# Huber loss on one core: the pair's target tile in parts of 8704 and 7680 columns instead of two rows

## The chip, the cores and the metric

The kernel runs on one core of a Trainium2 chip. The time of a run is the device time in microseconds (us). VectorE is called DVE in the profile and ScalarE ACT; SP is SyncE, which here only issues DMA transfers, and SPq is its queue of instructions. GB/s are 10^9 bytes a second, MB are 10^6 bytes; the profile's KB are 1024 bytes, so that 4096.0 KB are 4.19 MB.

## The reference

Two float32 arrays of 8192 x 8192 come in, one of the same shape goes out:

```python
def reference(pred, target):
    delta = 1.0
    diff = pred - target
    abs_diff = np.abs(diff)
    return np.where(abs_diff <= delta, 0.5 * diff**2, delta * (abs_diff - 0.5 * delta))
```

With d = pred - target the kernel computes max(|d| - 0.5, 0.5 * clip(d, -1, 1)**2), which is the same. Each input is read once and the output is written once: 536.87 MB in and 268.44 MB out.

## The kernel before

The 8192 rows are cut into 32 steps. A step has 256 rows, two neighbouring rows to each of the 128 partitions, so that a partition's share of a step lies in one run of 16,384 numbers (64 KB) in the DRAM. Step i's prediction is loaded into one of two buffers of that size, `pairs[i % 2]`. Its target is loaded into two buffers of one row each (8192 columns, 32 KB a partition): `rows[0]` for the even row, `rows[1]` for the odd one; there is only one of each, so the next step's target row can be loaded only when the present step's compute on it is over. The result is written over the prediction and stored from there as one transfer of 8.39 MB.

`compute(i, r, widths)` works on one row in pieces of columns. For each piece, DVE subtracts the target from the prediction in place (line 80, `tensor_tensor`) and writes the clipped difference over the target (line 81, `tensor_scalar`); ACT squares that with a scale (line 84) and takes the absolute value of the difference in place (line 85); DVE finishes with `max(|d| - 0.5, square)` (line 74, `scalar_tensor_tensor`). The list `todo` and `finish(2)` hold the last operation back by two pieces, so that DVE has subtracts to do while ACT works; `finish(0)` at the row's end does what is left. The pieces of an even row are `EVEN` (two of 4096 columns), those of an odd row `ODD` (4096, 2048, 2048), and both rows of the last step use `FINE` (four of 2048).

All transfers are issued by SP, and the order of the program is the order written by hand (`tc.manual_schedule()`, line 90). SP issues one after the other and stands still at one whose condition isn't met, with all later ones behind it. In the steady state, one step issues four transfers in this order:

- `load_row(i, 1)` (line 58): the odd target row of step i. It waits until step i-1's compute on `rows[1]` is over.
- `load_pair(i + 1)` (line 50): the next step's prediction. It waits until the store of step i-1, which used the same buffer, has ended.
- `load_row(i + 1, 0)` (line 58): the next even target row. It waits for step i's compute on `rows[0]`.
- `store_pair(i)` (line 61): it waits for step i's compute on its odd row.

Near the end the order differs a little. The last prediction is loaded a row at a time (lines 103 and 109, `load_pred_row`, line 54). The last odd target row is loaded in four pieces of 2048 columns (line 110), each of which waits only for the compute on its own columns. Then come the store of step 30 (line 112), that of the last step's even row (line 113) and four stores of 2048 columns of its odd row (line 114, `store_row`, line 66). At the start (lines 92 to 95), the first even row's prediction and target are loaded in two pieces each.

Of the kernel before, what the change touches and what calls it, by code (L numbers as in the profile page):

```python
# [1 line left out]

# [4 lines left out]


@with_exitstack
def kernel(  # L10
    ctx: ExitStack,
    tc: tile.TileContext,
    pred: bass.AP,
    target: bass.AP,
    out: bass.AP,
):
    nc = tc.nc
    P = 128
    R = 2
    fp32 = mybir.dt.float32  # L20
    Alu = mybir.AluOpType
    Act = mybir.ActivationFunctionType
    SQRT_HALF = 0.70710678118654752

    n_rows, W = pred.shape
    pred_t = pred.rearrange("(n p r) m -> n p (r m)", p=P, r=R)
    targ_t = target.rearrange("(n p r) m -> n p (r m)", p=P, r=R)
    out_t = out.rearrange("(n p r) m -> n p (r m)", p=P, r=R)
    n = pred_t.shape[0]

    pool = ctx.enter_context(tc.tile_pool(name="slots", bufs=1))
    pairs = [pool.tile([P, R * W], fp32, name=f"pair{k}") for k in range(2)]
    rows = [pool.tile([P, W], fp32, name=f"row{k}") for k in range(R)]

    EVEN = [4096, 4096]
    ODD = [4096, 2048, 2048]
    FINE = [2048, 2048, 2048, 2048]

    def cuts(widths):
        out_, at = [], 0  # L40
        for w in widths:
            out_.append(slice(at, at + w))
            at += w
        return out_

    def at_row(r, c):
        return slice(r * W + c.start, r * W + c.stop)

    def load_pair(i):
        nc.sync.dma_start(out=pairs[i % 2], in_=pred_t[i, :, :])  # L50

    def load_pred_row(i, r):
        c = slice(r * W, (r + 1) * W)
        nc.sync.dma_start(out=pairs[i % 2][:, c], in_=pred_t[i, :, c])  # L54

    def load_row(i, r, widths=None):
        for c in cuts(widths or [W]):
            nc.sync.dma_start(out=rows[r][:, c], in_=targ_t[i, :, at_row(r, c)])  # L58

    def store_pair(i):  # L60
        nc.sync.dma_start(out=out_t[i, :, :], in_=pairs[i % 2])  # L61

    def store_row(i, r, widths):
        for c in cuts(widths):
            ca = at_row(r, c)
            nc.sync.dma_start(out=out_t[i, :, ca], in_=pairs[i % 2][:, ca])

    def compute(i, r, widths):
        todo = []

        def finish(keep):
            while len(todo) > keep:
                a, b = todo.pop(0)
                nc.vector.scalar_tensor_tensor(  # L74
                    out=a, in0=a, scalar=-0.5, in1=b, op0=Alu.add, op1=Alu.max
                )

        for c in cuts(widths):
            a, b = pairs[i % 2][:, at_row(r, c)], rows[r][:, c]
            nc.vector.tensor_tensor(out=a, in0=a, in1=b, op=Alu.subtract)  # L80
            nc.vector.tensor_scalar(  # L81
                out=b, in0=a, scalar1=-1.0, scalar2=1.0, op0=Alu.max, op1=Alu.min
            )
            nc.scalar.activation(out=b, in_=b, func=Act.Square, scale=SQRT_HALF)  # L84
            nc.scalar.activation(out=a, in_=a, func=Act.Abs)  # L85
            todo.append((a, b))
            finish(2)
        finish(0)

    ctx.enter_context(tc.manual_schedule())  # L90

    for c in cuts(EVEN):
        nc.sync.dma_start(out=pairs[0][:, c], in_=pred_t[0, :, c])  # L93
        nc.sync.dma_start(out=rows[0][:, c], in_=targ_t[0, :, c])  # L94
    load_pred_row(0, 1)
    for i in range(n):
        last = i == n - 1
        if not last:
            load_row(i, 1)
            if i + 1 < n - 1:  # L100
                load_pair(i + 1)
            else:
                load_pred_row(i + 1, 0)
        compute(i, 0, EVEN if not last else FINE)
        if not last:
            load_row(i + 1, 0)
        compute(i, 1, ODD if not last else FINE)
        if i + 1 == n - 1:
            load_pred_row(i + 1, 1)
            load_row(i + 1, 1, FINE)  # L110
        if not last:
            store_pair(i)
    store_row(n - 1, 0, [W])
    store_row(n - 1, 1, FINE)


# [1 line left out]
_INS = ['pred', 'target']  # L118
_OUTS = [((8192, 8192), 'float32')]


# [23 lines left out]
```

## Time and profile before

| | us |
|---|---|
| median of 3 runs | 1877.39 |
| lowest and highest of them | 1874.84, 1877.78 |
| the profiled execution's own time | 1877.36 |
| its span | 1875.6 |
| ACT busy | 912.9 (49%) |
| SP's line 61 (store) waiting for DVE, in total | 798.2 |
| SP's line 50 (pair load) waiting for the store of two steps ago, in total | 710.6 |
| SP's line 58 (target load) waiting for DVE, in total | 227.6 |
| DVE waiting for a target load (line 80), in total | 306.7 |
| ACT waiting for DVE (line 84), in total | 948.5 |

The span is that of one execution, taken by the hardware profiler; the time of the same execution has 1.8 us more around it. Waiting times of different engines overlap, and a wait costs time only where nothing else is busy meanwhile. "DMA" in a view's row is the mean busy share of the core's 16 DMA engines; in short stretches it can pass 1.00, as a transfer's packets are counted where they begin.

The durations by operation and width (partitions x columns), which the prediction uses:

| line, operation | 128x4096, ns | 128x2048, ns |
|---|---|---|
| 80 TENSOR_TENSOR | 4423 | 2283 |
| 81 TENSOR_SCALAR | 2294 | 1226 |
| 84 ACTIVATE (square) | 3611 | 1894 |
| 74 SCALAR_TENSOR_TENSOR (STT) | 4424 | 2287 |

### The profile page before, as it was taken

To read this page: it belongs to the slowest core of one execution; us is meant where nothing else is said; L and a number is where in the kernel's file an instruction comes from. 1 tells how busy PE (TensorE), PEld (TensorE's weight loads), DVE (VectorE), ACT (ScalarE), POOL (GpSimd) and SP (SyncE) were. 2 spreads that over 40 slices of the span, in tenths; PEclk is the share of its full clock that TensorE was granted. 3 is DMA by queue.
4 is the path that set the end of the run, shared out by engine and by line. 5 is a ranking of instruction groups with operands and counts; after the bars stand their busy time and mean duration, and the time that the engine had idled before them with its cause. 6 is when DMAs were issued, how large, how long until landed. Compare 5 with 4: busy or idle time off the path is not lost.

```text
span 1875.6 us, 1196 instructions
## 1 busy us (share of the span) xinstructions
DVE 1430.2 (76%) x489; ACT 912.9 (49%) x327; POOL 0.2 (0%) x4
## 2 busy tenths in 40 slices
DVE  5777877778777787777877778777787777877787
ACT  3635536355364553644535445354453544535455
POOL 0000000000000000000000000000000000000000
DMA  9999999999999999999999999999999999999999
GB/s 425 414 436 435 438 425 429 439 428 431 440 425 442 429 429 442 419 434 443 417 436 432 439 425 426 425 442 427 428 428 442 424 427 443 418 435 423 428 425 386
DMA packets 20025, 805.39 MB, mean 429 GB/s; under 512 B 2224, under 2 KB 2224, under 8 KB 2224
## 3 DMA queue, kind: packets, MB, share of 16 engines
q1 hardware_dynamic: 20016, 805.32, 99.9%
q14 instruction: 9, 0.07, 0.0%
HBM read 536.87 MB, written 268.44 MB: 429 GB/s over the span
## 4 chain that ended last, share of the span: by engine, by line
DMA 57%; ACT 24%; DVE 17%; SPq 1%; issue 0%; DVEq 0%
DMA row<-in_target_dram 57%; ACT row L84 12%; ACT pair L85 12%; DVE pair L80 8%; DVE pair L74 4%; DVE row L81 4%; SPq L61 1%; DVEq L140 0%; SPq L94 0%; SPq L93 0%; SPq L58 0%; SPq L54 0%; DVEq L80 0%
## 5 line engine op out<-in xcount | busy, mean ns | idle before, releaser
L84 ACT ACTIVATE row<-row 128x4096 f32<-128x4096 f32 (+1 forms) x163 | 468.4, 2874 | 948.5 <-DVE row L81 948.5
L80 DVE TENSOR_TENSOR pair<-pair,row 128x4096 f32<-128x4096 f32 (+1 forms) x163 | 571.1, 3504 | 306.7 <-DMA row<-in_target_dram 306.7
L74 DVE SCALAR_TENSOR_TENSOR pair<-pair,row 128x4096 f32<-128x4096 f32 (+1 forms) x163 | 568.7, 3507 | 122.4 <-ACT pair L85 122.4
L85 ACT ACTIVATE pair<-pair 128x4096 f32<-128x4096 f32 (+1 forms) x163 | 467.4, 2867 | 0.0
L81 DVE TENSOR_SCALAR row<-pair 128x4096 f32<-128x4096 f32 (+1 forms) x163 | 299.1, 1835 | 5.6
L84 ACT ACT_TABLE_LOAD x1 | 1.3, 1283 | 0.7 <-PEq L129 0.7
L129 POOL MEMSET const-bfloat16-1.0<- 128x1 bf16 x1 | 0.1, 101 | 0.0
L129 POOL MEMSET const-uint8-127<- 128x1 uint8 x1 | 0.1, 101 | 0.0
L129 POOL MEMSET const-float32-0.0<- 128x1 f32 x1 | 0.1, 98 | 0.2 <-issue 0.2
L129 POOL MEMSET const-float32-1.0<- 128x1 f32 x1 | 0.1, 98 | 0.0
## 6 DMA issues: line engine op xcount, KB each, us to landing
row<-in_target_dram SPq DMA_DIRECT2D x62, 4096.0 KB, 33.9
pair<-in_pred_dram SPq DMA_DIRECT2D x3, 4096.0 KB, 29.7
pair<-in_pred_dram SPq DMA_DIRECT2D x2, 2048.0 KB, 11.6
row<-in_target_dram SPq DMA_DIRECT2D x2, 2048.0 KB, 16.1
row<-in_target_dram SPq DMA_DIRECT2D x4, 1024.0 KB, 15.7
out_dram<-pair SPq DMA_DIRECT2D x1, 4096.0 KB, 22.5
out_dram<-pair SPq DMA_DIRECT2D x4, 1024.0 KB, 9.5
out_dram<-pair SPq DMA_DIRECT2D x31, 25.3
```

Source lines behind the costliest of these rows:

```text
L61: nc.sync.dma_start(out=out_t[i, :, :], in_=pairs[i % 2])
L74: nc.vector.scalar_tensor_tensor(out=a, in0=a, scalar=-0.5, in1=b, op0=Alu.add, op1=Alu.max)
L80: nc.vector.tensor_tensor(out=a, in0=a, in1=b, op=Alu.subtract)
L81: nc.vector.tensor_scalar(out=b, in0=a, scalar1=-1.0, scalar2=1.0, op0=Alu.max, op1=Alu.min)
L84: nc.scalar.activation(out=b, in_=b, func=Act.Square, scale=SQRT_HALF)
L85: nc.scalar.activation(out=a, in_=a, func=Act.Abs)
L129: nc = _bacc.Bacc("TRN2", target_bir_lowering=False, num_devices=1)
```

## The change

The target's two buffers are no longer one row each. The pair of rows, which is one run of 16,384 columns, is cut at column 8704: part 0 has 8704 columns and part 1 has 7680. `targs[0]` and `targs[1]` have these sizes, 65,536 bytes a partition together as before. Compute goes by parts: part 0 in two pieces of 4352 columns, part 1 in pieces of 3840, 1920 and 1920; the last step in four pieces of 2176 and four of 1920. The pair buffers, the prediction loads and the stores of steps 0 to 29 stay as they were. In the last step the prediction comes in the two parts, the target's part 1 as one transfer instead of four, part 0 is stored as one transfer and part 1 in four of 1920 columns. The loop runs to the last step but one, and the last step's compute stands behind it.

```diff
+    CUT = 8704
+    part = [slice(0, CUT), slice(CUT, R * W)]
+    COARSE = [[4352, 4352], [3840, 1920, 1920]]
+    FINE = [[2176] * 4, [1920] * 4]
+
     pool = ctx.enter_context(tc.tile_pool(name="slots", bufs=1))
     pairs = [pool.tile([P, R * W], fp32, name=f"pair{k}") for k in range(2)]
-    rows = [pool.tile([P, W], fp32, name=f"row{k}") for k in range(R)]
+    targs = [
+        pool.tile([P, p.stop - p.start], fp32, name=f"targ{k}") for k, p in enumerate(part)
+    ]
 
-    EVEN = [4096, 4096]
-    ODD = [4096, 2048, 2048]
-    FINE = [2048, 2048, 2048, 2048]
...
+    def load_targ(i, k, widths=None):
+        for ca, cb in cuts(k, widths or [part[k].stop - part[k].start]):
+            nc.sync.dma_start(out=targs[k][:, cb], in_=targ_t[i, :, ca])
...
-    def compute(i, r, widths):
+    def compute(i, k, widths):
...
-        for c in cuts(widths):
-            a, b = pairs[i % 2][:, at_row(r, c)], rows[r][:, c]
+        for ca, cb in cuts(k, widths):
+            a, b = pairs[i % 2][:, ca], targs[k][:, cb]
...
-    for c in cuts(EVEN):
-        nc.sync.dma_start(out=pairs[0][:, c], in_=pred_t[0, :, c])
-        nc.sync.dma_start(out=rows[0][:, c], in_=targ_t[0, :, c])
-    load_pred_row(0, 1)
-    for i in range(n):
-        last = i == n - 1
-        if not last:
-            load_row(i, 1)
-            if i + 1 < n - 1:
-                load_pair(i + 1)
-            else:
-                load_pred_row(i + 1, 0)
-        compute(i, 0, EVEN if not last else FINE)
-        if not last:
-            load_row(i + 1, 0)
-        compute(i, 1, ODD if not last else FINE)
-        if i + 1 == n - 1:
-            load_pred_row(i + 1, 1)
-            load_row(i + 1, 1, FINE)
-        if not last:
-            store_pair(i)
-    store_row(n - 1, 0, [W])
-    store_row(n - 1, 1, FINE)
+    whole = slice(0, R * W)
+    for ca, cb in cuts(0, COARSE[0]):
+        load_pred(0, ca)
+        nc.sync.dma_start(out=targs[0][:, cb], in_=targ_t[0, :, ca])
+    load_pred(0, part[1])
+    for i in range(n - 1):
+        near_end = i + 1 == n - 1
+        load_targ(i, 1)
+        load_pred(i + 1, part[0] if near_end else whole)
+        compute(i, 0, COARSE[0])
+        load_targ(i + 1, 0)
+        compute(i, 1, COARSE[1])
+        if near_end:
+            load_pred(i + 1, part[1])
+            load_targ(i + 1, 1)
+        store(i, whole)
+    for k in range(2):
+        compute(n - 1, k, FINE[k])
+    store(n - 1, part[0])
+    for ca, _ in cuts(1, FINE[1]):
+        store(n - 1, ca)
```

`cuts(k, widths)` now gives each piece's columns twice, counted in the pair and in the part; `load_pred(i, c)` and `store(i, c)` move the columns `c` of a pair buffer.

More of the change, by code (lines that the diff above doesn't have):

```diff
@@ L29, with cuts, load_pred, store @@
     n = pred_t.shape[0]
+    CUT = 8704
+    part = [slice(0, CUT), slice(CUT, R * W)]
+    COARSE = [[4352, 4352], [3840, 1920, 1920]]
+    FINE = [[2176] * 4, [1920] * 4]
     pool = ctx.enter_context(tc.tile_pool(name="slots", bufs=1))
     pairs = [pool.tile([P, R * W], fp32, name=f"pair{k}") for k in range(2)]
-    rows = [pool.tile([P, W], fp32, name=f"row{k}") for k in range(R)]
-    EVEN = [4096, 4096]
-    ODD = [4096, 2048, 2048]
-    FINE = [2048, 2048, 2048, 2048]
-    def cuts(widths):
-        out_, at = [], 0
+    targs = [
+        pool.tile([P, p.stop - p.start], fp32, name=f"targ{k}") for k, p in enumerate(part)
+    ]
+    def cuts(k, widths):
+        at, found = 0, []
         for w in widths:
-            out_.append(slice(at, at + w))
+            found.append((slice(part[k].start + at, part[k].start + at + w), slice(at, at + w)))
             at += w
[L44 to L53, printed above, removed]
-        nc.sync.dma_start(out=pairs[i % 2][:, c], in_=pred_t[i, :, c])
[L56 to L63, printed above, removed]
-        for c in cuts(widths):
-            ca = at_row(r, c)
-            nc.sync.dma_start(out=out_t[i, :, ca], in_=pairs[i % 2][:, ca])
-    def compute(i, r, widths):
+        return found
+    def load_pred(i, c):
+        nc.sync.dma_start(out=pairs[i % 2][:, c], in_=pred_t[i, :, c])
+    def load_targ(i, k, widths=None):
+        for ca, cb in cuts(k, widths or [part[k].stop - part[k].start]):
+            nc.sync.dma_start(out=targs[k][:, cb], in_=targ_t[i, :, ca])
+    def store(i, c):
+        nc.sync.dma_start(out=out_t[i, :, c], in_=pairs[i % 2][:, c])
+    def compute(i, k, widths):
         todo = []
@@ L76, in finish @@
                 )
-        for c in cuts(widths):
-            a, b = pairs[i % 2][:, at_row(r, c)], rows[r][:, c]
+        for ca, cb in cuts(k, widths):
+            a, b = pairs[i % 2][:, ca], targs[k][:, cb]
             nc.vector.tensor_tensor(out=a, in0=a, in1=b, op=Alu.subtract)
```

## The prediction

> **What bounds the kernel now.** I read the page's head first, to see which engine is full.
>
> ```profile
> span 1875.6 us, 1196 instructions
> DVE 1430.2 (76%) x489; ACT 912.9 (49%) x327; POOL 0.2 (0%) x4
> ...
> DMA  9999999999999999999999999999999999999999
> ...
> q1 hardware_dynamic: 20016, 805.32, 99.9%
> ```
>
> The 16 DMA engines have work for 99.9% of the span; VectorE (DVE) has a quarter of it free. The page's chain blames target loads for 57% and compute for most of the rest, but a chain only follows what released what: a load that lands 34 us after its issue was queued most of that time. So I asked for stretches: all steps, then a quick step and a long one, then the end (columns: stretch, its length, three engines' busy time with counts, clock, DMA share, GB/s).
>
> ```profile
> 65.60:1820.10 1754.50, 1340.91 (x451) 853.78 (x300) 0.00 (x0) 1.00 1.00 431
> ```
>
> ```profile
> 592.20:650.20 58.00, 44.68 (x15) 28.46 (x10) 0.00 (x0) 1.00 1.00 432
> 650.20:709.40 59.20, 44.68 (x15) 28.46 (x10) 0.00 (x0) 1.00 1.00 434
> ```
>
> ```profile
> 1868.00:1870.00 2.00, 0.00 (x0) 0.00 (x0) 0.00 (x0) 1.00 1.00 422
> 1870.00:1872.00 2.00, 0.00 (x0) 0.00 (x0) 0.00 (x0) 1.00 0.53 221
> 1872.00:1874.00 2.00, 0.00 (x0) 0.00 (x0) 0.00 (x0) 1.00 0.15 61
> ```
>
> Compute is identical in short and long steps; only the stream's length differs. The DMA engines stay full to 1870 us, five microseconds after the last compute, and then stop one by one over some 4 us: they don't run level, and the last one sets the end. Last, the timeline of one step, to see how early each transfer is queued (start, duration, engine, line; in brackets the idle time before it).
>
> ```profile
> 1702.38 0.34 SPq L61 DMA_DIRECT2D out_dram<-pair  x1
> 1702.83 0.37 SPq L58 DMA_DIRECT2D row<-in_target_dram  x1
> 1709.23 4.42 DVE L80 TENSOR_TENSOR pair<-pair,row 128x4096 f32<-128x4096 f32 x1 [6.87 <-DMA row<-in_target_dram]
> ...
> 1728.50 0.33 SPq L50 DMA_DIRECT2D pair<-in_pred_dram  x1
> ...
> 1734.63 0.33 SPq L58 DMA_DIRECT2D row<-in_target_dram  x1
> 1738.20 4.42 DVE L80 TENSOR_TENSOR pair<-pair,row 128x4096 f32<-128x4096 f32 x1 [3.59 <-DMA row<-in_target_dram]
> ...
> 1761.66 0.34 SPq L61 DMA_DIRECT2D out_dram<-pair  x1
> ```
>
> Transfers run in the order SyncE (SP) issued them. The store issued at 1702.38 finds the even row's target load still running; that lands at 1709.23, so the store had 6.9 us of **cover** (time by which a transfer is queued before the engines need it). The pair load, which waits for that store, is issued at 1728.50 with the odd row's target load still ahead of it until 1738.20: 9.7 us of cover. The kernel is bound by its stream of bytes; compute matters only if a cover runs out.
>
> **The change, part by part.** The sum is made against this execution's own 1877.36 us (span 1875.6 and 1.8 around it), practically the median of the runs, 1877.39.
>
> *Bytes.* Same 805.3 MB, same sizes of prediction loads and of stores but for the last. Per step the stream is 25.17 MB; at 431 GB/s that is 58.4 us before and after: 0.
>
> *Target loads.* Part 0 has 4.456 MB and takes 10.34 us at that rate, part 1 3.932 MB and 9.12 us, against 9.73 each: +0.61 and -0.61, sum 0. What no row shows is a run of 34,816 or 30,720 bytes a partition. The nearest are at the start: between the first compute at 12.91 us and the second at 22.68, 4.19 MB in runs of 16 KB came (429.3 GB/s); to the third at 42.12, 8.39 MB in runs of 32 KB (431.5). Halving the run costs 0.5%. Taken as the bound for both signs on target bytes, a third of all: 0.5% of 625 us, so 3.1 us more or less. I take 0, because the new runs differ by 6% from 32 KB, one longer and one shorter.
>
> *Fewer transfers.* The last target load goes as one transfer, not four, and three fewer in all. The four last 1 MB stores run at 418 to 430 GB/s between 1864 and 1870; 2% of their 9.8 us is 0.2 us for four, so -0.1 us for three; between 0 and -0.2.
>
> *Narrower and wider pieces.* As many instructions over as many columns. From the groups by form: TENSOR_TENSOR takes 4423 ns at 4096 columns and 2283 at 2048, so 1.045 ns a column and 0.14 us fixed; SCALAR_TENSOR_TENSOR 4424 and 2287 the same; TENSOR_SCALAR 2294 and 1226, 0.52 a column; ACTIVATE 3611 and 1894, 0.84. Part 0's path is a subtract, a clip, four ACTIVATEs and a last STT: at 256 columns more, 0.27+0.13+4x0.215+0.27 = 1.53 us, so 25.40 (1709.23 to 1734.63) becomes 26.93. Part 1's path (subtract, clip and two ACTIVATEs of 4096 less 256, four ACTIVATEs and an STT of 2048 less 128) shrinks by 0.27+0.13+0.43+0.43+0.13 = 1.39: 23.45 becomes 22.06. All of it lies beside the stream. The covers that hide it:
>
> - Store: part 1 is done 1.39 earlier, the load in front of it lasts 0.61 longer: 5.7 to 6.9 us becomes 7.7 to 8.9. The next target load is behind the store on SP and gains too.
> - Pair load: only part 1's load lies ahead of it, 9.7 becomes 9.1. Behind it on SP stands part 0's next load, which waits for part 0's compute (6.1 us later) and is needed only when the pair load ends, 19.5 us after 1738.2: some 23 us, now 21.
> - DVE between the parts: its 3.59 idle shrinks by 1.53+0.61 to 1.4. If that went, part 1 would start late by the excess and use up the store's cover; first cost beyond 1.4+7.7 = 9.1 us.
>
> So 0. Without the store's cover every microsecond late would be paid 31 times.
>
> *Start.* Part 0's two first pieces land 0.6 and 1.2 us later (22.68 to 23.9). By the durations above part 0 ends at 43.4 instead of 41.05, part 1 starts then instead of 42.12 and ends at 65.5; the first store was issued at 65.58 and covered until 72.1. 0.
>
> *End.* The whole target load of the last pair waits for all of part 1's compute; its first piece went at 1814.66, the new one goes at 1796.26+22.06 = 1818.3, and the prediction load ahead of it runs to about 1825.4 (1796.24 plus 29.2 us for 12.58 MB): still covered by 7 us. It lands near 1835.2, where the last compute of part 1 wants it at 1818.3+24.07 = 1842.4 (22.73 us and 1.34 for 128 columns more in four rounds). The last piece is done at 1863.8 instead of 1865.0; the stream ahead of it lasts to about 1872. 0.
>
> The Trainium skill ("DMA: Bandwidth & Descriptors", section on measured bandwidth) speaks against the new last stores: it asks for 1 MiB or more a transfer and gives a lone 1 MB load, issued from GpSimd, 6.15 us at 341 GB/s; the pieces fall below that size. The rows above show four of them at 418 to 430 GB/s in the queue; by the page's figure the four would take 24.6 us and the end would come some 15 us later in both kernels, which the trace before contradicts.
>
> Sum: 0 + 0 - 0.1 + 0 = -0.1: **1877.3 us**.
>
> **Rivals.**
>
> *The stream gets smoother (faster).* Steps last 58.05 us at best (592.2 to 650.2) and 58.49 on average ((1761.66-65.58)/29). If the 2 us of cover given to the store took away half of what separates them, 31x0.22 = 6.8 us would go: 1870.5. For it: engines up to 4 us ahead of the last have only some 2 of the store's 5.7 us. Against: they aren't the ones that set the end, and the long step before 709.4 shows full DMA share. 13%.
>
> *The cut at 8704 streams worse (slower).* Place: the 62 target loads, whose second part now starts 34,816 bytes into a partition's 65,536. It decides from a loss of 0.6% on them (3.75 us); at double the bound, 6.2 us: 1883.5. For it: no such run has been seen. Against: the engines moved 16, 32 and 64 KB runs within 0.5% of each other. 11%.
>
> *A cover runs out at the pair load (slower).* The engine that sets the end would have to need it 9.1 us earlier than this trace has it; then 31 us for each microsecond beyond. The widest spread seen, 4 us, is far off. 2%, near 1890.
>
> *The change doesn't do what it says.* The last transfers stand in their old order but for four loads made one, so "another order" may be worth nothing at all: inside the forecast.
>
> **How the numbers follow.** The forecast has 74%. Its own range is the bound of 3.1 us and the runs' spread (1874.84 to 1877.78) together: 1873.5 to 1880.7. The range reaches a little into both rivals: 1872.0 to 1881.5. What a measurement here can tell from no change is about 0.2%, 3.75 us. Faster 14% (the smoother stream and a tail of the forecast), slower 13%, within 73%.
>
> **What would show it.** DMA stays at 99.9% and 431 GB/s through the steps; the store's cover (idle before part 0's first subtract plus its wait) grows by 2 us; idle between the parts falls to about 1.4; DVE busy stays at 1430 us; the last compute ends 1.2 us earlier and the span doesn't. It is wrong if steps lose DMA share, or if target loads alone take more than 10.4 and 9.2 us.

## The result and the profile after

| | before | after |
|---|---|---|
| median, us | 1877.37 (6 runs, 1874.84 to 1878.47) | 1870.81 (6 runs, 1869.23 to 1871.98) |
| profiled execution, its own time and span, us | 1877.36, 1875.6 | 1869.80, 1868.0 |

The changed kernel takes 0.9966 of the time before, with a 95% interval of 0.9953 to 0.9979: 6.6 us less. The forecast was 1877.3 us, its range 1872.0 to 1881.5. The measured time lies where the first rival put it (1870.5).

The page of the changed kernel, its head and its DMA queue:

```profile
span 1868.0 us, 1192 instructions
DVE 1430.3 (77%) x489; ACT 912.9 (49%) x327; POOL 0.2 (0%) x4
...
q1 hardware_dynamic: 19584, 805.32, 99.9%
```

Bytes, busy times and the share of 99.9% are as before, and still 7.6 us are gone from the span. A busy share can't show this: an engine that takes longer over a packet is as busy as one that doesn't. The stretches tell where it went: all steps, a quick step and a long one.

```profile
65.50:1812.10 1746.60, 1341.04 (x451) 853.79 (x300) 0.00 (x0) 1.00 1.00 433
647.80:705.80 58.00, 44.67 (x15) 28.46 (x10) 0.00 (x0) 1.00 1.00 432
938.60:997.40 58.80, 44.69 (x15) 28.46 (x10) 0.00 (x0) 1.00 1.01 432
```

From the first store to that of step 30 it is 1746.6 us, where the kernel before took 1754.5 (65.6 to 1820.1): 433 GB/s instead of 431. From store to store, 17 of the 30 steps take less than 58.2 us, 9 before, and the longest takes 58.8 us instead of 59.4. But for the first (57.5 us) the quick ones are no quicker than before (58.05); there are more of them. What follows the last of these stores takes 55.9 us (1812.1 to 1868.0), before 55.5. So, counted from store issue to store issue, the whole gain is in the steps, and none at the end, whose order had changed. The engines still stop one by one:

```profile
1860.00:1862.00 2.00, 0.00 (x0) 0.00 (x0) 0.00 (x0) 1.00 1.02 430
1862.00:1864.00 2.00, 0.00 (x0) 0.00 (x0) 0.00 (x0) 1.00 0.88 369
1864.00:1866.00 2.00, 0.00 (x0) 0.00 (x0) 0.00 (x0) 1.00 0.31 131
```

The timeline of a step, beside that of the prediction (start, duration, engine, line; idle time in brackets):

```profile
1695.68 0.34 SPq L57 DMA_DIRECT2D out_dram<-pair  x1
1696.12 0.38 SPq L54 DMA_DIRECT2D targ<-in_target_dram  x1
1703.31 4.69 DVE L71 TENSOR_TENSOR pair<-pair,targ 128x4352 f32<-128x4352 f32 x1 [7.66 <-DMA targ<-in_target_dram]
...
1722.55 0.33 SPq L50 DMA_DIRECT2D pair<-in_pred_dram  x1
...
1730.24 0.33 SPq L54 DMA_DIRECT2D targ<-in_target_dram  x1
1731.64 4.16 DVE L71 TENSOR_TENSOR pair<-pair,targ 128x3840 f32<-128x3840 f32 x1 [1.42 <-DMA targ<-in_target_dram]
```

DVE sits idle for 7.66 us between the store's issue and the landing of part 0: that idle time is the store's cover, read off the line. Over the 30 stores its median is 7.7 us; before it was 5.9 (5.7 to 6.9). The reader sees an engine idle for longer in a kernel that is faster.

**Engine by engine.** The trace has the start, duration and size of each DMA packet. A partition's run is one packet, and a transfer gives each engine eight of them and a completion of 4 bytes. On an engine one packet follows the last almost always within 10 ns, so the 16 engines can be told apart by following ends to starts. A packet of 65,536 bytes takes 2.418 us (median), of 32,768 1.213, of 34,816 1.288, of 30,720 1.138. What a packet takes beyond its size's median is called its stall here. The next table, worked out from the packets, puts the whole-pair stores of each kernel into classes by how long after SP's issue an engine began with the store, and gives the mean stall in the rest of that store and in the load behind it, with the number of cases in brackets:

```
begun after issue by   0-1 us     1-1.5      1.5-2      2-3       over 3 us
before                 853 (36)   678 (49)   200 (137)  48 (54)   25 (204)   ns
e1, cut at 8192        791 (25)   662 (64)   214 (121)  60 (68)   16 (202)
e3, later store        -          586 (57)   259 (138)  45 (99)   57 (186)
e5, cut at 7680       1031 (32)   905 (128)  356 (136) 101 (140) 221 (44)
after                  -          -          -          -          8 (480)
e2, earlier store      -          -          -          -          9 (480)
```

Before, 46% of the cases began within 2 us of the issue, the engines that run ahead above all; with them the last packet of the store, 18 us after its issue, took up to a microsecond longer. After, in this execution, no case began within 3 us. Times begun are counted from the issue: in 29 of the 480 cases before, the engine stood empty when the store was issued, and its first packet came 0.84 to 1.02 us later. So the first class is mostly engines without any cover left, and a case of 1.5 us had some 0.6 us of slack.

This stall alone is 0.206 us a step on the mean engine before and 0.008 after: 30 x 0.198 = 5.9 us. The mean engine ended at 1871.46 us before and at 1864.58 after, 6.9 earlier; the last one at 1874.34 and 1866.87. Two smaller losses are gone too: engines that stood empty ahead of a store (0.5 us on the mean engine) and stalls in the last target load (0.6).

### The profile page after: what moved, and what is told of

It reads as the page before. It is cut to its first block, busy times and chain, and to the rows that moved or that the text cites. A ratio compares the mean times of both kernels' runs of the same rounds, so it can differ in the third digit from the quotient of the medians.

```text
span 1868.0 us, 1192 instructions
## 1 busy us (share of the span) xinstructions
DVE 1430.3 (77%) x489; ACT 912.9 (49%) x327; POOL 0.2 (0%) x4
## 2 busy tenths in 40 slices
DMA packets 19593, 805.39 MB, mean 431 GB/s; under 512 B 2176, under 2 KB 2176, under 8 KB 2688
## 3 DMA queue, kind: packets, MB, share of 16 engines
q1 hardware_dynamic: 19584, 805.32, 99.9%
## 4 chain that ended last, share of the span: by engine, by line
DMA 58%; ACT 23%; DVE 17%; SPq 1%; issue 0%; DVEq 0%
DMA targ<-in_target_dram 58%; ACT targ L75 11%; ACT pair L76 11%; DVE pair L71 8%; DVE pair L65 5%; DVE targ L72 4%; SPq L57 1%; DVEq L129 0%; SPq L50 0%; SPq L54 0%; SPq L86 0%; DVEq L71 0%
## 5 line engine op out<-in xcount | busy, mean ns | idle before, releaser
L75 ACT ACTIVATE targ<-targ 128x1920 f32<-128x1920 f32 (+3 forms) x163 | 468.5, 2874 | 940.8 <-DVE targ L72 934.4
L71 DVE TENSOR_TENSOR pair<-pair,targ 128x1920 f32<-128x1920 f32 (+3 forms) x163 | 571.2, 3505 | 294.7 <-DMA targ<-in_target_dram 294.7
L65 DVE SCALAR_TENSOR_TENSOR pair<-pair,targ 128x1920 f32<-128x1920 f32 (+3 forms) x163 | 568.8, 3507 | 126.4 <-ACT pair L76 126.4
L76 ACT ACTIVATE pair<-pair 128x1920 f32<-128x1920 f32 (+3 forms) x163 | 467.3, 2867 | 0.0
L72 DVE TENSOR_SCALAR targ<-pair 128x1920 f32<-128x1920 f32 (+3 forms) x163 | 299.2, 1835 | 5.6
```

Of the source, the lines that this page charges most:

```text
L65: nc.vector.scalar_tensor_tensor(out=a, in0=a, scalar=-0.5, in1=b, op0=Alu.add, op1=Alu.max)
L72: nc.vector.tensor_scalar(out=b, in0=a, scalar1=-1.0, scalar2=1.0, op0=Alu.max, op1=Alu.min)
```

## The experiments

Three theories stood against each other. A: the store's longer cover. B: the cut itself, that is the new length and place of the target's runs. C: the end of the program. All ratios are against the kernel before on the same chip; its medians there were 1876.06 (e1 to e4), 1876.03 (e5 to e8) and 1875.84 us (e9 to e11).

| run | store's cover, median of 30 stores, us | median time, us | ratio, 95% interval |
|---|---|---|---|
| e5, cut at 7680 | 3.8 | 1881.92 | 1.0029, 1.0018 to 1.0039 |
| before | 5.9 | | 1 |
| e1, cut at 8192 | 5.9 | 1875.91 | 0.9997, 0.9988 to 1.0005 |
| e3, later store | 6.1 | 1874.26 | 0.9986, 0.9977 to 0.9995 |
| e10, the changed kernel again | 7.7 | 1870.07 | 0.9968, 0.9956 to 0.9981 |
| e2, before with an earlier store | 8.6 | 1869.77 | 0.9966, 0.9954 to 0.9979 |
| e6, cut at 9216 | 9.7 | 1870.20 | 0.9966, 0.9954 to 0.9979 |
| e7, cut at 9728 | 10.6 | 1871.53 | 0.9971, 0.9959 to 0.9982 |

**e1: the cut put back.**

```diff
-    CUT = 8704
+    CUT = 8192
-    COARSE = [[4352, 4352], [3840, 1920, 1920]]
-    FINE = [[2176] * 4, [1920] * 4]
+    COARSE = [[4096, 4096], [4096, 2048, 2048]]
+    FINE = [[2048] * 4, [2048] * 4]
```

> The changed kernel with the cut put back to column 8192 and the pieces to 4096 and 2048 columns; its end (last target load as one transfer) stays. The store's cover is then that of the kernel before, 5.7 us. Theory A (the store's cover of 7.7 us keeps engines that run ahead from being held back): 1877 us. Theory B (the new place and length of the target runs make the change from store to load smoother): 1877 us. Theory C (the end of the program gained it): 1871 us.

1875.91 us, the time before. Its step's store and the first subtract behind it:

```profile
1702.57 0.34 SPq L57 DMA_DIRECT2D out_dram<-pair  x1
...
1708.24 4.42 DVE L71 TENSOR_TENSOR pair<-pair,targ 128x4096 f32<-128x4096 f32 x1 [5.70 <-DMA targ<-in_target_dram]
```

The cover is back at 5.70 in this step (median 5.9), and with it the time. The end has the new order, so that order alone doesn't bring the gain. One of its 11 runs took 1869.55 us, as little as the changed kernel; the others lie between 1873.83 and 1877.81. By the packets the stores account for 5.7 us of the mean engine's loss against the changed kernel, and the last target load, begun 1.0 us after its issue, for 1.7 us more.

**e2: the kernel before with an earlier store.**

```diff
             nc.scalar.activation(out=b, in_=b, func=Act.Square, scale=SQRT_HALF)
+            if widths is ODD and c.stop == W:
+                continue
             nc.scalar.activation(out=a, in_=a, func=Act.Abs)
```

> The kernel before, with two operations left out for the last 2048 columns of each odd row (all but the last step's): the absolute value and the final operation, so that the output is wrong there by design of the test and part 1's compute is about 2.9 us shorter. Every transfer is unchanged; the store's cover rises from 5.7 to about 8.6 us. Theory A: 1869 to 1872 us. Theories B and C: 1877 us, as no transfer has changed.

1869.77 us, with every transfer that of the kernel before:

```profile
1693.05 0.34 SPq L61 DMA_DIRECT2D out_dram<-pair  x1
...
1701.56 4.42 DVE L80 TENSOR_TENSOR pair<-pair,row 128x4096 f32<-128x4096 f32 x1 [8.55 <-DMA row<-in_target_dram]
```

The work it leaves out was beside the stream in any case; what it changes for the stream is the moment of the store's issue. That brings the whole gain, without a new cut and with the old end: theory B isn't needed, and theory C falls. (The load behind the store goes earlier with it; e9 below tests that one apart.)

**e3: the changed kernel with a later store.**

```diff
-    COARSE = [[4352, 4352], [3840, 1920, 1920]]
+    COARSE = [[4352, 4352], [3840, 3840]]
```

> The changed kernel with part 1 in two pieces of 3840 instead of 3840, 1920 and 1920. Its compute ends about 1.8 us later (23.8 us instead of 22.1), so the store's cover falls from 7.7 back to about 5.9 us, while all transfers stay. Theory A: 1875 to 1877 us. Theories B and C: 1871 us.

1874.26 us, over half of the way back, a little less than theory A's bounds. The cover came out at 6.17 us in this step, not 5.9:

```profile
1700.63 0.34 SPq L57 DMA_DIRECT2D out_dram<-pair  x1
...
1706.78 4.69 DVE L71 TENSOR_TENSOR pair<-pair,targ 128x4352 f32<-128x4352 f32 x1 [6.17 <-DMA targ<-in_target_dram]
```

Its median over the stores is 6.1 us, hardly above e1's, and 41% of the cases began within 2 us (e1: 44%); of the difference in time, 0.7 us on the mean engine lies in the last target load (1.1 against 1.7). So e3 tells less than the table's order suggests. Its 11 runs lie from 1869.56 to 1876.03, more widely than those of the changed kernel (1869.03 to 1873.19 with e10's). It may hang on the run how many engines get ahead far enough to meet a late store; with one trace of it that isn't shown.

**e5: the cut the other way.**

```diff
-    CUT = 8704
+    CUT = 7680
-    COARSE = [[4352, 4352], [3840, 1920, 1920]]
-    FINE = [[2176] * 4, [1920] * 4]
+    COARSE = [[3840, 3840], [4352, 2176, 2176]]
+    FINE = [[1920] * 4, [2176] * 4]
```

> The changed kernel with the cut the other way, at column 7680: part 0 in two pieces of 3840 columns, part 1 in 4352, 2176 and 2176. Part 1's compute takes 24.8 us and the load in front of the store 9.1, so the store's cover falls to 3.7 us, below the kernel before (5.7). Theory A (late stores hold back the engines that run ahead, and every engine ends later): slower than before, 1879 to 1890 us. Theory B (a cut away from the rows' border makes the transfers smoother, whatever the cover): 1871 us.

1881.92 us, slower than before. The same two sizes of target runs in the other order, and the sign turns:

```profile
1707.16 0.34 SPq L57 DMA_DIRECT2D out_dram<-pair  x1
...
1710.86 4.16 DVE L71 TENSOR_TENSOR pair<-pair,targ 128x3840 f32<-128x3840 f32 x1 [3.72 <-DMA targ<-in_target_dram]
```

3.72 us of cover, 62% of the cases within 2 us of the issue, and the largest stalls of the table. The last target load, begun 1.6 us after its issue, cost 1.2 us besides. DMA's share in this page is 99.9% again.

**e6 and e7: more cover.** The cut at 9216 and at 9728; e7 has the numbers of its expectation.

```diff
-    CUT = 8704
-    COARSE = [[4352, 4352], [3840, 1920, 1920]]
-    FINE = [[2176] * 4, [1920] * 4]
+    CUT = 9216
+    COARSE = [[2304, 4608, 2304], [3584, 1792, 1792]]
+    FINE = [[2304] * 4, [1792] * 4]
```

> The changed kernel with the cut at column 9216, part 0 in pieces of 2304, 4608 and 2304 (so that its longer compute is over before part 1's target lands), part 1 in 3584, 1792 and 1792. Store's cover some 9.7 us instead of 7.7, the pair load's 8.5 instead of 9.1. Theory A: as fast as the changed kernel or up to 3 us faster, 1867 to 1871 us. If the pair load's cover counts as the store's does: slower than 1871 us.

> The same with the cut at column 9728 (2432, 4864, 2432 and 3328, 1664, 1664): store's cover some 11.3 us, the pair load's 7.9. Theory A: as e6 within 2 us, the gain is used up once no engine starts a store within 2 us of its issue. If the pair load's cover counts: slower than e6.

1870.20 and 1871.53 us. A step's store and the first subtract behind it, in e6 and in e7:

```profile
1693.76 0.34 SPq L57 DMA_DIRECT2D out_dram<-pair  x1
...
1703.40 2.56 DVE L71 TENSOR_TENSOR pair<-pair,targ 128x2304 f32<-128x2304 f32 x1 [9.66 <-DMA targ<-in_target_dram]
```

```profile
1692.68 0.34 SPq L57 DMA_DIRECT2D out_dram<-pair  x1
...
1703.22 2.69 DVE L71 TENSOR_TENSOR pair<-pair,targ 128x2432 f32<-128x2432 f32 x1 [10.57 <-DMA targ<-in_target_dram]
```

e7's cover came out at 10.6 us, not 11.3. Nothing more is to be had than with 7.7, and the pair load's shorter cover costs nothing that shows. By the packets, the mean engine ends earlier still (1863.45 and 1862.72 us), but the engines end further apart and the last one doesn't follow (1867.17 and 1866.37; after: 1864.58 and 1866.87).

**e4 and e8: the store in two.** Part 0's half is issued before part 1's compute; e8 leaves step 30's store whole.

```diff
         load_targ(i + 1, 0)
+        store(i, part[0])
         compute(i, 1, COARSE[1])
...
-        store(i, whole)
+        store(i, part[1])
```

> The changed kernel with each pair's store in two: part 0's as soon as its compute is over, part 1's after part 1's compute. The first has a cover of some 20 us, the second about 17 us, but there are 31 transfers more, at some 0.05 us each (1.6 us) or a little more. Theory A: below the changed kernel, 1866 to 1870 us. Theories B and C: 1872 to 1874 us, slower by the added transfers.

> The split stores of e4 but for the last one but one, step 30's, which is stored whole, so that the last step's loads aren't queued behind half a store. e4's last stores stood with empty engines near the end (1.9 us on average). Theory A: 1.5 to 2 us below e4, 1868 to 1870 us.

1870.91 us (0.9974, 0.9964 to 0.9985) and 1872.12 us (0.9977, 0.9967 to 0.9987). e4 is just outside its bounds, e8 is a miss. In e4 the engines stood empty for 1.9 us on the mean before the last stores, whose compute came too late. The added transfers cost more than I had put down: two packets of half the size take 8 ns longer than one (2 x 1.213 against 2.418 us), and with a completion of 9 ns each that is 8 x 8 + 9 = 73 ns a transfer on each engine, 2.3 us for 31. In e8 no engine stood empty before a store, but the mean engine lost 1.3 us in the last target load instead, ahead of the whole store: the first engine began that load 1.1 us after its issue, in the changed kernel's first trace 3.5 us after it, without loss. Its engines ended 4.0 us apart from mean to last (1865.10 and 1869.12); why so far stays open.

**e9: a late load behind an early store.**

```diff
             nc.vector.tensor_tensor(out=a, in0=a, in1=b, op=Alu.subtract)
+            if then and ca.start == 0:
+                then()
...
-        load_targ(i, 1)
-        load_pred(i + 1, part[0] if near_end else whole)
-        compute(i, 0, COARSE[0])
+        def then():
+            if i:
+                nc.vector.memset(targs[1][:, 0:1], 0.0)
+            load_targ(i, 1)
+            load_pred(i + 1, part[0] if near_end else whole)
+
+        compute(i, 0, COARSE[0], then)
```

> The changed kernel, its store as early as there (cover 7.7 us), but the target load behind the store held back: it waits for a tiny write of one column into its buffer that DVE makes after part 0's first subtract, some 12.5 us after the store's issue instead of 0.45. The store (19.5 us) still covers it by more than 10 us. If it is the store that must not come late (A1): 1870 to 1872 us. If it is the load behind it that the engines must know of when they begin the store (A2): stalls at the stores' ends as in the kernel before, 1876 to 1880 us.

1870.49 us (0.9968, 0.9956 to 0.998). The load behind the store, line 54, is issued 12.9 us after it instead of 0.44:

```profile
1696.16 0.34 SPq L57 DMA_DIRECT2D out_dram<-pair  x1
1704.26 4.69 DVE L71 TENSOR_TENSOR pair<-pair,targ 128x4352 f32<-128x4352 f32 x1 [8.13 <-DMA targ<-in_target_dram]
1708.90 0.06 DVE L95 MEMSET targ<- 128x1 f32 x1
...
1709.04 0.33 SPq L54 DMA_DIRECT2D targ<-in_target_dram  x1
```

All engines had begun the store by then (at the latest 8.0 us after its issue), and it cost nothing: e10, the changed kernel on the same chip, took 1870.07 us. It is the store's own issue that must not be late; the load behind it need not be queued yet when the engines begin the store, though the stall shows where the one meets the other.

**e10 and e11: the changed kernel again, and with part 0 in three pieces.**

```diff
-    COARSE = [[4352, 4352], [3840, 1920, 1920]]
+    COARSE = [[2176, 4352, 2176], [3840, 1920, 1920]]
```

> The changed kernel itself, once more, beside e9 and e11 on their chip: 1871 us by every theory.

> The changed kernel with part 0 in pieces of 2176, 4352 and 2176 columns: its compute ends some 3 us earlier, so DVE's idle time between the parts grows from about 1.4 us, and the next part-0 load is issued earlier; the store's cover and every transfer stay. Theory A: 1871 us, as only the store's cover counts. If DVE's scarce time between the parts is what leaves the changed kernel above 1869: 1868 to 1869 us.

1870.07 and 1870.08 us (e11: 0.9963, 0.9951 to 0.9976). DVE's idle time between the parts rose to 3.68 us, the store's cover stayed at 7.67, and the time stayed with it:

```profile
1701.51 2.42 DVE L71 TENSOR_TENSOR pair<-pair,targ 128x2176 f32<-128x2176 f32 x1 [7.67 <-DMA targ<-in_target_dram]
...
1730.64 4.16 DVE L71 TENSOR_TENSOR pair<-pair,targ 128x3840 f32<-128x3840 f32 x1 [3.68 <-DMA targ<-in_target_dram]
```

e10's trace also shows how much the spread of the engines differs between executions of the same kernel: with the same cover, 25 of its 480 cases began a store within 2 us of the issue, 0.03 us a step on the mean engine, and the last target load, begun 1.5 us after its issue, cost 0.9 us. That execution took 1871.23 us, the one profiled first 1869.80.

No version tried beats the changed kernel beyond its interval.

## Why the prediction was wrong

- *Durations and stages: right.* Part 0 takes 26.93 us (1703.31 to 1730.24), as worked out; part 1 22.07 (1731.64 to 1753.71) against 22.06. The idle time between the parts is 1.42 us against 1.4, the store's cover 7.66 against 7.7, the first store's issue 65.5 as forecast, DVE's busy time 1430.3. The signs that missed are those of the stream: 433 GB/s instead of 431, and a last compute that ends 7.9 us earlier (1857.1 us), with the span 7.6 us shorter.
- *Target runs: right at 0.* 34,816 and 30,720 bytes take 1.288 and 1.138 us, in proportion to 32,768 in 1.213. The argument that 16, 32 and 64 KB runs go "within 0.5% of each other" was a little short: by the packets (0.611, 1.213 and 2.418 us) the first is 1.1% slower than the last. The rival of the worse cut falls with e1, e2 and e5: the sign follows the cover, not the cut. The rival at the pair load falls with e6 and e7.
- *End and fewer transfers: right about the end's length* (55.9 us for 55.5); the packets' medians add up to 0.2 us less on an engine, for the 0.1 put down. The last target load was forecast to land at 1835.2 us; by the forecast's own 1825.4 and 9.12 it is 1834.5, which changes nothing. "Still covered by 7 us" was again the last engine's cover (7.2 us); the first engine had 3.5 us, and in e10 1.5 us. The last stores, of 0.98 MB, run at 430 GB/s from 1860 to 1862. The Trainium skill ("DMA: Bandwidth & Descriptors", section on measured bandwidth) asks for transfers of at least 1 MiB to reach 75% of the peak; these pieces, which stood in a queue, lost nothing that shows.
- *The step that failed* is "All of it lies beside the stream ... So 0", in its first line, the store: "5.7 to 6.9 us becomes 7.7 to 8.9". I weighed that cover against zero, for the last engine, and called the added 2 us worth nothing. But engines that ran some 4 us ahead of the last had only 1 to 2 us of the 5.7, and those stalled. The cover had a price for them before it was used up (29 of the 222 cases within 2 us had none left): 0.2 us a step on the mean engine, up to 1 us on one.
- *The rival that came true* gave 13% to just this mechanism and 6.8 us to it; 6.6 were measured. Its "half of what separates them" was a guess that no row carried, so that the size came so near is in part luck. The argument against it, that the engines ahead "aren't the ones that set the end", is what misled. By the packets it holds for single stalls and not for the sum. Before, most engines lost 5 to 8 us each at the ends of the 30 stores; the few others, the last to end, lost 6 to 12 us in the target loads just ahead of the stores. After, the losses ahead of the stores are 2.7 to 7.1 us over all engines. That an early store cures the first kind is shown by e1, e2 and e5. The second kind isn't cured: it is 4.1 us on the mean engine before and 4.6 after, only no longer heaped on the engines that end last. Why it is spread out so, and where it comes from, stays open.
- *The chances.* 73% for no change was too much. Steps of 58.0 and 59.2 us with the same compute were shown and then taken as given; 0.2 us in each of 30 steps is 6 us, more than the 3.75 that tell a change from none.

## What to carry to other kernels

A transfer's cover is not the same for all DMA engines: take off what the engines ahead are early (look at how gradually they stop at the end) and ask for 2 us or more on top of that, not for more than nothing. Look at more than one execution: the engines' spread changes from one to the next (e10). In a kernel at 99.9% DMA share, compare the lengths of equal steps: if they differ, the stream itself loses time, and moving work from the stage in front of a late store to another with idle time can win it back without a byte less. Once every engine has its store in time, more cover brought nothing here (e6, e7).

## What the runs showed of the hardware that was not expected

- A store begun within 1.5 us of its issue costs an engine 0.6 to 1.0 us, not at its start but in its last packet or the first of the load behind it, some 18 us later; between 2 and 3 us it costs 0.05 to 0.1 us. Beyond 3 us next to nothing is left, but for e5, whose 44 cases there still have 0.2 us; that is not explained.
- One load shows the same. The last target load is issued just ahead of step 30's store. Where its first engine began it 1.0 to 1.8 us after the issue (e1, e3, e5, e8, e9, e10), the mean engine lost 0.7 to 1.7 us in it; where that was 2.4 us or more (the changed kernel's first trace, e4, e6, e7, e11), 0.02 to 0.06 us. No run changed this alone. The next pair's load can't tell: no engine began it sooner than 2.3 us after its issue in any run.
- The 16 engines drift apart: the first load's 16 completions come within 0.3 us before and 0.5 after, the last store's within 3.8 and 3.7. The Trainium skill ("DMA: Bandwidth & Descriptors", on why a DMA increments its semaphore by 16) says that the engines of one transfer finish independently, and these numbers agree.
